# A hybrid attention and short-convolution block on one core: the order of its start, the steps of its attention, and how one row of scales is spread over the partitions

## The chip, the cores and the metric

The kernel runs on one core of a Trainium2 chip. The metric is the device time of one execution in microseconds. The engines are named as the profile names them: PE is TensorE (matmuls), PEld its weight load, DVE VectorE, ACT ScalarE, POOL GpSimd, and SP is SyncE, whose queue issues nearly all DMA transfers here. Each engine takes its own instructions in the order in which the program holds them, and one that waits holds up all that stand behind it on the same engine.

## The reference

One layer of a diffusion block over 512 latent tokens (width 2048) with 256 context tokens, everything in fp32:

```
mod_l = silu(c) @ w_ada + b_ada            # 6 x 2048 numbers: shifts, scales, gates
mod_c = silu(c_ctx) @ w_ada + b_ada
h_l = rms_norm(x, g) * (1 + sc_a) + sh_a   # h_c likewise from ctx
qa, kva, kr, cb, cc, ch = split(h @ w_in)
q = rms_norm(qa) @ w_q_b ;  k, v = rms_norm(kva) @ w_kv_b      # 8 heads, rotary part shared
att = softmax(q k^T * scale) v             # 512 queries, 768 keys
conv = cb * dwconv3(cc * ch)
x = x + gt_a * (rms_norm_per_128(concat(att, conv)) @ w_out)
hf = rms_norm(x) * (1 + sc_f) + sh_f
u = dwconv3(hf @ w_up); x = x + gt_f * ((a * silu(g)) @ w_down)
return rms_norm(x, g_final)
```

## The kernel before, in words

The activations lie transposed in the core's memory: 16 tiles of 128 features by 512 tokens. Every fp32 operand of a large product is split into a high part (a cast on ACT to the matmul's own 32-bit format, name ending in h) and a low part (a subtraction on DVE, name ending in l), and `mm3` makes three matmuls of each product, high by high, high by low and low by high (L170 to L172). So a weight block that has landed still needs one ACT and one DVE instruction before PE can use it whole.

**The start.** c lands, four matmuls spread it over the partitions, ACT applies silu to it (`silu_rows`), and sv holds it. Sixteen tiles of x (xr) land; ACT squares each (L317 ff.), DVE adds the squares into one tile xs0t (L318), and PE sums that over the partitions into rs (L283). In between PE and ACT do the same for c_ctx (tile cc, into svc). `rsqrt` takes the root on ACT and the reciprocal on DVE, `spread` (L264) turns the 512 numbers into a tile rl with equal rows: a matmul of a broadcast column with the identity for every 128 tokens. With rl each x tile j is scaled (`modulate`, L398), given its scale and shift (ACT, L401) and split into hj. The scale and shift of tile j are two of the 96 products of w_ada with sv: a *dot* is a DVE instruction over 128x1024 numbers that multiplies a landed half tile of w_ada with half of sv and sums it (`dot_v`, L216), so two halves for each product. The halves land in a ring of four buffers (tag ada), and SP issues all transfers in program order (`ordered`, L128), so a transfer behind a half waits until the dot that frees its buffer is done. The input projection runs over the 16 tiles in three chunks of k (2, 6 and 8 tiles; the names pf, rf, wf belong to a chunk's first columns, pp, rw, w to the others), and w_in comes in pieces of up to 1 MB in a ring of two buffers (tag raw, three in later parts).

**The attention** (from about 444 us) has 32 steps: a head and a quarter of the queries each. A step takes the row maximum of the scores from PSUM (DVE, L683), multiplies it by -scale (DVE, L684), applies exp (ACT, L687), transposes the six 128x128 blocks of the probabilities on PE (t, L700), splits them into pth (ACT, L703) and ptl (DVE, L704), computes scores two steps ahead, and every second step multiplies by the values (po). Beside that, each step does one *late dot* pair (ra, L238), loads the next 1 MB of w_ada for it in three of every four steps, does one eighth of the next head pair's projections (`pieces`), and fetches one step ahead the weights that this will use (rq, rk, `fetch`). After each head pair `merge` spreads eight groups of scales (gr) with the matmuls of L741 into gb; `gn_apply` (late_bg) does so for the convolution groups by `spread` (gn).

**After the last step** comes the output projection (of): its operands mx0 to mx15 are split (L300, L301), its first weights (ofr into ofw) are fetched and split, and dots go on (ada). Which instruction an engine takes next where the program leaves it open is set by the scheduler that builds the program; `keep` pins an instruction to program order.

Of the kernel before, what the change touches and what calls it, by code (L numbers as in the profile page):

```python
# [60 lines left out]
def block_kernel(ctx, tc, xt, ctxt, ctxn, c, c_ctx, w_ada, small, w_in, w_inc, w_q, w_kv, w_out,  # L61
# [67 lines left out]

    def fetch_to(dst, src):  # L130

        ins = SP.dma_start(dst, src)
        if ordered[0]:
            keep(ins)
# [10 lines left out]
    def split(raw, a, n, name):  # L145
# [7 lines left out]
        A.copy(out=hi[:, :n], in_=raw[:, a:a + n])  # L153
        V.tensor_tensor(out=lo[:, :n], in0=raw[:, a:a + n], in1=hi[:, :n].bitcast(F32), op=ALU.subtract)  # L154
# [53 lines left out]
    def total(col, t, dst):  # L208

        V.scalar_tensor_tensor(out=dst, in0=col[:, 0:1], scalar=col[:, 1:2], in1=s("b_ada", t), op0=ALU.add, op1=ALU.add)  # L210

    def dot_v(raw, vec, t, dst, nm):

        col = tiny(2, f"dv{nm}{t}")
        for i, r in enumerate(raw):
            V.scalar_tensor_tensor(out=r, in0=r, scalar=1.0, in1=vec[:, i * 1024:(i + 1) * 1024], op0=ALU.mult, op1=ALU.mult, accum_out=col[:, i:i + 1])  # L216
# [39 lines left out]
    def scale_of(dst, g, m):  # L256
        V.scalar_tensor_tensor(out=dst, in0=m, scalar=1.0, in1=g, op0=ALU.add, op1=ALU.mult)

    def rsqrt(r, ms, n):

        A.activation(r, ms, AF.Sqrt, bias=eps, scale=1.0 / n)
        V.reciprocal(r, r)

    def spread(pb, r):  # L264

        for g in range(r.shape[1]):
            PE.matmul(pb[:, g * P:(g + 1) * P], bc(r[:, g:g + 1], P), ident, start=True, stop=True)

    def rms_steps(sqs, n, a, width, dst, wait=0, one=False):
# [11 lines left out]
        for i, sq in enumerate(sqs):  # L281
            for g in range(ng):
                PE.matmul(ps[:, g:g + 1], sq[:, a + g * P:a + (g + 1) * P], ones[:, 0:1], start=i == 0 and g == 0, stop=i == len(sqs) - 1 and g == ng - 1)  # L283
# [5 lines left out]
        if dst is not None:  # L289
            A.copy(out=dst[:, a:a + width], in_=pb[:, :width])  # L290
        yield pb[:, :width]

    def rms(sqs, n, width, dst):
        for _ in rms_steps(sqs, n, 0, width, dst):
            pass

    def hilo(src, n, nm, width=512):
        hi = t2([P, width], F32R, nm + "h")
        lo = t2([P, width], F32R, nm + "l")
        A.copy(out=hi[:, :n], in_=src)  # L300
        V.tensor_tensor(out=lo[:, :n], in0=src, in1=hi[:, :n].bitcast(F32), op=ALU.subtract)  # L301
# [8 lines left out]
    def add_squares(total, x, n, nm, E=None, a=0, new=tmp):  # L310
        c = slice(a, a + n)
        if total is None:
            total = new([P, T], F32, nm + "t")
            A.activation(total[:, c], x, AF.Square)
            return total
        q = tmp([P, T], F32, nm)
        A.activation(q[:, :n], x, AF.Square)  # L317
        (E or V).tensor_tensor(out=total[:, c], in0=total[:, c], in1=q[:, :n], op=ALU.add)  # L318
# [44 lines left out]
    with ExitStack() as pa:  # L363
# [4 lines left out]
        def silu_rows(src, dst, nm):  # L368
# [3 lines left out]
            for g in range(4):  # L372
# [4 lines left out]
                A.activation(dst[:, g * 512:(g + 1) * 512], ps, AF.Silu)  # L377

        def ada_load(t):
            return ada_tiles(p_sb, 4, w_ada[t], f"ada{t}")  # L380

# [8 lines left out]

        def prep(j):
# [934 lines left out]
```

## Time and profile before

| | us |
|---|---|
| Median of 3 runs | 2210.82 |
| Lowest, highest | 2207.34, 2219.75 |
| The profiled execution: its time | 2206.8 |
| The profiled execution: its span | 2204.9 |
| Granted clock of PE in it | 0.996 |
| ACT, POOL busy | 1010.5, 111.3 |

The span is what the trace covers; 1.9 us of that execution's time lie outside it. The median of the runs lies 4.0 us above the profiled execution. A row of the timeline has the start, the length, the engine, the line, the operation, the tiles (result on the left of the arrow) and how many instructions it stands for, and in brackets the idle time ahead of it and what ended that. Matmuls overlap, so the length of one says less than the distance between the starts of two.

### The profile page before, as it was taken

To read this page: it belongs to the slowest core of one execution; us is meant where nothing else is said; L and a number is where in the kernel's file an instruction comes from. 1 tells how busy PE (TensorE), PEld (TensorE's weight loads), DVE (VectorE), ACT (ScalarE), POOL (GpSimd) and SP (SyncE) were. 2 spreads that over 40 slices of the span, in tenths; PEclk is the share of its full clock that TensorE was granted. 3 is DMA by queue.
4 is the path that set the end of the run, shared out by engine and by line. 5 is a ranking of instruction groups with operands and counts; after the bars stand their busy time and mean duration, and the time that the engine had idled before them with its cause. 6 is when DMAs were issued, how large, how long until landed. Compare 5 with 4: busy or idle time off the path is not lost.

```text
span 2204.9 us, 34542 instructions
## 1 busy us (share of the span) xinstructions
PE 2149.2 (97%) x13346; PEld 1914.2 (87%) x13346; DVE 1599.0 (73%) x2493; ACT 1010.5 (46%) x1635; POOL 111.3 (5%) x149
## 2 busy tenths in 40 slices
PE   7899999999999999999999999999999999999998
PEld 4688888878888888899999999999999888888887
DVE  7998887678896848777777777777777873633544
ACT  5523333544452237555554555555554432532444
POOL 0000000000000000011111011111110000000000
PEclk9999999999999999999999999999999999999999
DMA  8989884434469925577777777777776995753462
GB/s 331 344 276 334 275 279 150 144 120 149 158 235 358 331 86 172 132 196 201 204 194 195 201 205 195 194 201 201 201 193 200 350 345 159 247 164 92 160 210 88
DMA packets 144264, 466.75 MB, mean 212 GB/s; under 512 B 16290, under 2 KB 20642, under 8 KB 138082
## 3 DMA queue, kind: packets, MB, share of 16 engines
q1 hardware_dynamic: 125652, 405.03, 54.1%
q0 software_dynamic: 16272, 57.42, 12.8%
q8 instruction: 104, 1.70, 0.3%
q10 hardware_dynamic: 2176, 2.10, 0.3%
q14 instruction: 60, 0.49, 0.1%
HBM read 442.73 MB, written 20.71 MB: 210 GB/s over the span
## 4 chain that ended last, share of the span: by engine, by line
PE 91%; DVE 4%; DMA 2%; ACT 2%; issue 1%; SPq 0%; POOL 0%; DVEq 0%; ACTq 0%
PE d L170 7%; PE d L172 7%; PE d L171 7%; PE pp L170 4%; PE pp L172 4%; PE pp L171 4%; PE o L172 1%; PE o L171 1%; PE o L170 1%; PE uf L170 1%; PE uf L171 1%; PE uf L172 1%; PE of L172 1%; PE pf L171 1%; PE of L170 1%; PE of L171 1%
## 5 line engine op out<-in xcount | busy, mean ns | idle before, releaser
L997 POOL DMA_DIRECT2D u_s<-in_w_up x80 | 68.1, 851 | 416.3 <-DMA u_s<-in_w_up 353.4
L153 ACT CAST w_0h<-rw 128x512 fp32r<-128x512 f32 (+1 forms) x63 | 38.5, 618 | 107.3 <-PE pp L171 65.7
L216 DVE SCALAR_TENSOR_TENSOR ada<-ada,sv 128x1024 f32<-128x1024 f32 x64 | 77.4, 1217 | 4.6 <-DMA ada<-in_w_ada 4.6
L491 DVE SCALAR_TENSOR_TENSOR ada<-ada,svc 128x1024 f32<-128x1024 f32 x64 | 75.9, 1218 | 2.0 <-DMA ada<-in_w_ada 1.8
L238 DVE SCALAR_TENSOR_TENSOR ra<-ra,sv 128x1024 f32<-128x1024 f32 x50 | 59.4, 1216 | 0.0
L154 DVE TENSOR_TENSOR w_0l<-rw,w_0h 128x512 fp32r<-128x512 f32 (+1 forms) x63 | 42.4, 680 | 21.8 <-ACT w_0h L153 21.8
L238 DVE SCALAR_TENSOR_TENSOR ada<-ada,sv 128x1024 f32<-128x1024 f32 x46 | 55.7, 1218 | 2.6 <-DMA ada<-in_w_ada 2.6
L1108 DVE TENSOR_TENSOR u<-u,u 128x1024 f32<-128x1024 f32 x40 | 49.0, 1225 | 1.3
L1107 DVE TENSOR_TENSOR u<-u,u_s 128x1024 f32<-128x1024 f32 x40 | 48.7, 1217 | 0.0
L939 POOL DMA_DIRECT2D y_d<-a x43 | 24.7, 576 | 386.2 <-DVE a L938 376.7
L732 POOL TENSOR_TENSOR gr<-gr,half 128x8 f32<-128x8 f32 x4 | 8.3, 2084 | 641.4 <-DVE mx L684 505.3
L238 DVE SCALAR_TENSOR_TENSOR adl<-adl,sv 128x1024 f32<-128x1024 f32 x32 | 38.8, 1218 | 0.2 <-DMA adl<-in_w_ada 0.2
L683 DVE TENSOR_REDUCE mx<-s 128x1 f32<-128x768 f32 x32 | 30.4, 951 | 8.4 <-PE s L673 8.4
L704 DVE TENSOR_TENSOR ptl<-t,pth 128x384 fp32r<-128x384 f32 x64 | 33.2, 548 | 4.2 <-ACT pth L703 4.2
L502 DVE TENSOR_TENSOR acc<-acc,pp 128x512 f32<-128x512 f32 x50 | 33.9, 678 | 1.9 <-PE pp L172 1.8
L703 ACT CAST pth<-t 128x384 fp32r<-128x384 f32 x64 | 28.5, 488 | 14.3 <-PE t L700 14.1
L936 ACT ACTIVATE g<-g 128x512 f32<-128x512 f32 x43 | 27.2, 633 | 12.1 <-DVE g L930 12.1
L928 ACT ACTIVATE g<-cg,sm 128x512 f32<-128x512 f32 x40 | 32.5, 813 | 0.0
L687 ACT ACTIVATE p<-s,mx 128x768 f32<-128x768 f32 x32 | 29.3, 915 | 6.8 <-DVE mx L684 6.6
L928 ACT ACTIVATE a<-ca,sm 128x512 f32<-128x512 f32 x40 | 32.1, 802 | 0.0
L700 PE MATMUL t<-io,p 128*128 128x128 f32 x192 | 27.5, 274 | 3.7 <-ACT p L687 2.4
L929 DVE SCALAR_TENSOR_TENSOR g<-cg,sm,g 128x511 f32<-128x511 f32 x40 | 29.8, 745 | 0.0
(15580 smaller groups left out, 8734.8 us busy)
## 6 DMA issues: line engine op xcount, KB each, us to landing
ada<-in_w_ada SPq DMA_DIRECT2D x174, 512.0 KB, 6.0
u<-in_w_up SPq DMA_DIRECT2D x120, 512.0 KB, 8.3
u_s<-in_w_up SPq DMA_DIRECT2D x80, 512.0 KB, 4.1
u_s<-in_w_up POOLq DMA_DIRECT2D x80, 512.0 KB, 9.5
d<-in_w_dn SPq DMA_DIRECT2D x86, 384.0 KB, 3.8
y<-y_d SPq DMA_DIRECT2D x129, 256.0 KB, 4.5
ra<-in_w_ada SPq DMA_DIRECT2D x25, 1024.0 KB, 4.8
adl<-in_w_ada SPq DMA_DIRECT2D x32, 512.0 KB, 6.0
```

The lines of the kernel that those rows point to most:

```text
L153: A.copy(out=hi[:, :n], in_=raw[:, a:a + n])
L154: V.tensor_tensor(out=lo[:, :n], in0=raw[:, a:a + n], in1=hi[:, :n].bitcast(F32), op=ALU.subtract)
L170: PE.matmul(ps, w[0], x[0], start=first, stop=False, skip_group_check=on_top)
L171: PE.matmul(ps, w[0], x[1], start=False, stop=False, skip_group_check=on_top)
L172: PE.matmul(ps, w[1], x[0], start=False, stop=last, skip_group_check=on_top)
L216: V.scalar_tensor_tensor(out=r, in0=r, scalar=1.0, in1=vec[:, i * 1024:(i + 1) * 1024], op0=ALU.mult, op1=ALU.mult, accum_out=col[:, i:i + 1])
L238: keep(V.scalar_tensor_tensor(out=r, in0=r, scalar=1.0, in1=svs[i], op0=ALU.mult, op1=ALU.mult, accum_out=lc[:, t % 4:t % 4 + 1] if i else ...
L491: keep(V.scalar_tensor_tensor(out=raw[q], in0=raw[q], scalar=1.0, in1=svc[:, q * 1024:(q + 1) * 1024], op0=ALU.mult, op1=ALU.mult, accum_o ...
L928: A.activation(u, src, AF.Identity, bias=s("fb", m), scale=s("fw", 86 + m))
L997: G_.dma_start(r[-1], src[more], accum_op=ALU.add)
L1107: V.tensor_tensor(out=a11, in0=a11, in1=s1, op=ALU.add)
L1108: V.tensor_tensor(out=a12, in0=a12, in1=a11, op=ALU.add)
```

## The change

It has six parts.

1. **Spreads.** `spread` issues a PE transpose of the broadcast column where it had a matmul with the identity. `merge` now calls `spread` too.
2. **The start.** The dots of tiles 0 and 1 (products 16, 0, 17, 1) get buffers of their own, four quarters of 128x512 each, with quarters' dots (`ada_quarter`); those of 16 land ahead of x, those of 0, 17 and 1 after the first weights. DVE's, ACT's and SP's order in this stretch is written out and pinned (`pin`). The squares are added in groups of five tiles (xs0t, xs5t, xs10t, xs15t), and PE sums each group over the partitions as it is done. A small silu and the constant sm come early; a root no longer stands between.
3. **c_ctx.** The PE spread of c_ctx is gone. After the first weights of chunk 1 (rf12) a DMA broadcasts c_ctx to all partitions (128x2048, 1 MB), and one ACT silu of 128x2048 makes svc of it.
4. **A root and exp tables.** A tiny exp after the last root of the stretch before the attention.
5. **Softmax.** g_q is multiplied by -scale once, so that the scores come out negated and scaled; the step takes the row minimum, and the multiplication L684 goes.
6. **Steps.** The first q_nope of the second pair is done ahead of the loop, weights are fetched up to two steps ahead, and the late loads stand in steps 2 to 7 of every eight, so that steps 0 and 1 have none and the dots of steps 1 and 2 of every eight are gone.
The diff, cut to its core:

```diff
@@ spread, rms_steps
-            PE.matmul(pb[:, g * P:(g + 1) * P], bc(r[:, g:g + 1], P), ident, start=True, stop=True)
+            PE.transpose(pb[:, g * P:(g + 1) * P], bc(r[:, g:g + 1], P), ident)
@@ the start
+        def ada_quarters(t):
+            r = []
+            for i in range(4):
+                r.append(t2([P, T], F32, f"aq{t}{i}"))
+                fetch_to(r[i], w_ada[t][:, i * T:(i + 1) * T])
+            return r, tiny(4, f"dq{t}")
...
+        fetch_to(sm, small)
+        quarters = {16: ada_quarters(16)}
         xs = []
-        for j in range(NK):
-            xs.append(t2([P, T], F32, f"xr{j}"))
-            fetch_to(xs[j], xt[:, j * T:(j + 1) * T])
-            ssq = add_squares(ssq, xs[j], T, f"xs{j}")
-        silu_rows(c_ctx, svc, "cc")
-        fetch_to(sm, small)
-        rms([ssq], D, T, rl)
+        def squares():
+            for j in range(NK):
+                xs.append(t2([P, T], F32, f"xr{j}"))
+                fetch_to(xs[j], xt[:, j * T:(j + 1) * T])
+                ssq = add_squares(ssq if j % 5 else None, xs[j], T, f"xs{j}")
+                if j in (1, 3, 5):
+                    next(silus)
+                if j in (6, 8, 11, 13):
+                    ada_quarter(16)
+                if j % 5 == 4 or j == NK - 1:
+                    yield ssq
+        rms(squares(), D, T, rl, 4)
+        first_raw = load(w_in[:, :2 * G * P], 2 * G * P, "rf00")
+        quarters.update({t: ada_quarters(t) for t in (0, 17, 1)})
+        ada_quarter(0)
+        first_w = blocks(first_raw, 4, "wf00")
+        ada_quarter(0)
+        normed(0)
+        ada_quarter(0)
+        ada_quarter(0)
+        modulate(0)
+        first_w += blocks(first_raw, 8, "wf04", 4)
+        for t in (17, 1):
+            for _ in range(4):
+                ada_quarter(t)
+        normed(1)
+        modulate(1)
@@ after chunk 1's first columns
+                fetch_to(svc, c_ctx.to_broadcast([P, D]))
+                A.activation(svc, svc, AF.Silu)
                 fetch_to(kc, consts[:, :KCW])
@@ softmax
-            V.tensor_reduce(mx, ss[:, :768], axis=AX.X, op=ALU.max)
-            V.tensor_scalar(mx, mx, scalar1=-SCALE, scalar2=None, op0=ALU.mult)
+            V.tensor_reduce(mn, ss[:, :768], axis=AX.X, op=ALU.min)
-            A.activation(pt, ss[:, :768], AF.Exp, bias=mx, scale=SCALE, accum_out=den[hd // 2][:, i:i + 1])
+            A.activation(pt, ss[:, :768], AF.Exp, bias=mn, scale=-1.0, accum_out=den[hd // 2][:, i:i + 1])
@@ the attention's loop
-            if n % 4 != 3:
-                late_load(ada_raw)
-            if pr < 3:
-                f, p_, i = pieces(pr + 1)[n % 8]
-                f(p_, i)
-                if n + 1 < 24:
-                    fetch((n + 1) // 8 + 1, (n + 1) % 8)
+            at = n % 8
+            if at == 0 and n and n < 24:
+                fetch(pr + 1, 1)
+            if pr < 3 and n:
+                f, p_, i = pieces(pr + 1)[at]
+                f(p_, i)
+            if at < 2 and n < 24:
+                fetch(pr + 1, 2 + at)
+            elif at >= 2:
+                late_load(ada_raw)
+                if at == 6 and n < 16:
+                    fetch(pr + 2, 0)
```

The order of the instructions follows. The first place is DVE between the reciprocal of the root and the low part of tile 0 (h0l). aq and ada are pieces of w_ada under a dot, wf the split first weights, xr the x tile scaled by rl. Before:

```order
L262 RECIPROCAL rr<-rr 128x4
L154 TENSOR_TENSOR wf_0l<-rf_249,wf_0h 128x512
L154 TENSOR_TENSOR wf_4l<-rf_249,wf_4h 128x512
L154 TENSOR_TENSOR wf_8l<-rf_249,wf_8h 128x512
L398 TENSOR_TENSOR xr_112<-xr_112,rl 128x512
L216 SCALAR_TENSOR_TENSOR ada_281,dvl_285<-ada_281,sv 128x1024
L301 TENSOR_TENSOR h0l<-xr_112,h0h 128x512
```

In the changed kernel the same stretch of DVE reads:

```order
L279 RECIPROCAL rr<-rr 128x4
L415 SCALAR_TENSOR_TENSOR aq_233,dq_241<-aq_233,sv 128x512
L165 TENSOR_TENSOR wf_0l<-rf_231,wf_0h 128x512
L415 SCALAR_TENSOR_TENSOR aq_235,dq_241<-aq_235,sv 128x512
L430 TENSOR_TENSOR xr_118<-xr_118,rl 128x512
L415 SCALAR_TENSOR_TENSOR aq_237,dq_241<-aq_237,sv 128x512
L415 SCALAR_TENSOR_TENSOR aq_239,dq_241<-aq_239,sv 128x512
L417 TENSOR_TENSOR dq_241<-dq_241 128x2
L221 SCALAR_TENSOR_TENSOR mod<-dq_241,sm 128x1
L270 SCALAR_TENSOR_TENSOR sc_271<-mod,sm 128x1
L321 TENSOR_TENSOR h0l<-xr_118,h0h 128x512
```

The four dots of product 0 moved from ahead of the reciprocal to behind it, and two of them stand between the scaling of x and the scale sc that tile 0 needs.

The second place is DVE after the attention: from the last ptl (the last low part of a transposed block) to the first low weights of the output projection, ofw_0l. Before, all that stands between is this:

```order
L704 TENSOR_TENSOR ptl_5856<-t_5902,pth_5855 128x3x128
L301 TENSOR_TENSOR mx2l<-acc_393,mx2h 128x512
L301 TENSOR_TENSOR mx3l<-acc_423,mx3h 128x512
L243 TENSOR_TENSOR mod<-mod,lc 128x4
L238 SCALAR_TENSOR_TENSOR ra_5894,mod<-ra_5894,sv 128x1024
L244 TENSOR_TENSOR mod<-mod,sm 128x4
L238 SCALAR_TENSOR_TENSOR ra_5894,lc<-ra_5894,sv 128x1024
L154 TENSOR_TENSOR ofw_0l<-ofr_5997,ofw_0h 128x512
```

In the changed kernel 33 instructions stand between the two: the low parts mx1l to mx13l, six dots of ra, four of ada, the scalings of four acc and two o by gb, and four of a few numbers each. The last twelve rows up to ofw_0l read:

```order
L321 TENSOR_TENSOR mx7l<-acc_736,mx7h 128x512
L820 SCALAR_TENSOR_TENSOR o_5707<-o_5707,sm,gb_5970 128x512
L251 SCALAR_TENSOR_TENSOR ada_6061,mod<-ada_6061,sv 128x1024
L321 TENSOR_TENSOR mx8l<-o_4126,mx8h 128x512
L820 SCALAR_TENSOR_TENSOR o_5866<-o_5866,sm,gb_5976 128x512
L321 TENSOR_TENSOR mx9l<-o_4384,mx9h 128x512
L251 SCALAR_TENSOR_TENSOR ada_6063,lc<-ada_6063,sv 128x1024
L321 TENSOR_TENSOR mx10l<-o_4673,mx10h 128x512
L321 TENSOR_TENSOR mx11l<-o_4931,mx11h 128x512
L321 TENSOR_TENSOR mx12l<-o_5222,mx12h 128x512
L321 TENSOR_TENSOR mx13l<-o_5480,mx13h 128x512
L165 TENSOR_TENSOR ofw_0l<-ofr_5995,ofw_0h 128x512
```

The split of the first output weights moved behind the splits of nearly all operands and behind eight more dots.

The third place is PE at the same point. Before, two groups of spreads (gb) are left, and of starts with a piece whose low weights follow at once. Now all spreads stand ahead and these rows follow:

```order
L284 MATMUL gb_5976<-io,gr_5941 128x128 x4
L181 MATMUL of_5990<-mx0h,ofw_0h 128x512
L182 MATMUL of_5990<-mx0l,ofw_0h 128x512
L181 MATMUL of_5991<-mx0h,ofw_0h 128x512
L182 MATMUL of_5991<-mx0l,ofw_0h 128x512
L181 MATMUL of_5994<-mx0h,ofw_4h 128x512
L182 MATMUL of_5994<-mx0l,ofw_4h 128x512
L181 MATMUL of_5992<-mx0h,ofw_0h 128x512
L182 MATMUL of_5992<-mx0l,ofw_0h 128x512
L181 MATMUL of_5993<-mx0h,ofw_0h 128x512
L182 MATMUL of_5993<-mx0l,ofw_0h 128x512
L183 MATMUL of_5990<-mx0h,ofw_0l 128x512
```

Ten matmuls moved ahead of the first one that needs ofw_0l. On ACT the broadcast's silu stands, with a table load ahead of it, between the casts wf_0h and wf_4h of chunk 1's last first weights (rf12).

96 lines of the change are left out of this document (65 added, 31 removed).

## The prediction

> **What bounds the kernel now.** I read the page first, then the windows, then the waits of PE by stretch, and last the timelines of the two places at which the change puts DVE's work in another order. From the page come the busy times and the chain that ended last:
>
> ```profile
> PE 2149.2 (97%) x13346; PEld 1914.2 (87%) x13346; DVE 1599.0 (73%) x2493; ACT 1010.5 (46%) x1635; POOL 111.3 (5%) x149
> PE 91%; DVE 4%; DMA 2%; ACT 2%; issue 1%; SPq 0%; POOL 0%; DVEq 0%; ACTq 0%
> ```
>
> PE is the bound: whatever shortens its own work or ends its waits shows in full, and whatever only relieves DVE shows nothing, unless PE waits for DVE. The windows (microseconds, then busy time and count of PE, PEld, DVE, ACT and POOL, PE's clock, DMA share, GB/s) tell where PE is not dense:
>
> ```profile
> 0.00:30.00 30.00, 18.55 (x32) 8.25 (x32) 19.48 (x35) 20.91 (x35) 0.20 (x4) 1.00 0.95 356
> 85.00:410.00 325.00, 323.23 (x1429) 261.70 (x1428) 282.56 (x543) 119.48 (x216) 0.00 (x0) 1.00 0.75 259
> 410.00:636.00 226.00, 212.26 (x1448) 191.56 (x1446) 179.12 (x353) 112.49 (x244) 5.79 (x3) 1.00 0.43 148
> 636.00:670.00 34.00, 32.81 (x171) 27.73 (x172) 34.00 (x62) 14.39 (x26) 2.55 (x1) 0.95 0.87 311
> ```
>
> From 85 us to the attention PE is full, so a start that ends later by some microseconds stays late. Up to 636 us it idles 226.00 - 212.26 = 13.7 us; behind that DVE is busy all 34 us of its window. PE's waits between 410 and 670 us (total, times, longest):
>
> ```profile
> PE s L669 <- ACT p L687: 3.4, 3, 1.5
> PE t L700 <- ACT p L687: 2.4, 2, 2.1
> PE pq L172 <- DVE wq12l L154: 1.3, 1, 1.3
> PE pq L170 <- ACT wq11h L153: 0.9, 1, 0.9
> PE qr L342 <- ACT xq L591: 0.7, 1, 0.7
> PE pq L170 <- ACT wq21h L153: 0.5, 1, 0.5
> ```
>
> **Term 1, the start: +6 us.** The timelines of DVE, ACT and PE around the root:
>
> ```profile
> 18.09 1.49 DVE L318 TENSOR_TENSOR xs0t<-xs0t,xs 128x512 f32<-128x512 f32 x2
> 22.73 1.87 PE L283 MATMUL rs<-io,xs0t 128*128 128x1 f32 x8
> 27.38 0.59 ACT L290 COPY rl<-rs 128x512 f32<-128x512 f32 x1 [0.83 <-PE rs L267]
> 28.00 0.69 DVE L398 TENSOR_TENSOR xr<-xr,rl 128x512 f32<-128x512 f32 x1 [0.56 <-ACT rl L290]
> 28.73 0.81 ACT L401 ACTIVATE xr<-xr,mod,sc 128x512 f32<-128x512 f32 x1 [0.76 <-DVE xr L398]
> 29.57 0.62 ACT L300 CAST h0h<-xr 128x512 fp32r<-128x512 f32 x1
> 30.24 2.08 PE L170 MATMUL pf<-h0h,wf_0h 128*128 128x512 f32 x4 [2.90 <-ACT h0h L300]
> ```
>
> The adds end at 19.58; PE, still at the spread of c_ctx, comes to the sum at 22.73. Without that spread the sum would start with the last add. But ahead of x now come 1 MB of quarters and the constants, some 1.3 MB, at the 356 GB/s of the first window 3.5 us; I put the last add at 22 (19.6 if x had slack, 23 if all 3.5 count). Two groups of sums are left then, 2 x 1.87, and root, reciprocal, spread and copy take 27.97 - 24.60 = 3.4 less some 0.8 for the shorter spread (term 3): with 22 + 3.74 + 2.6 rl is ready at 28.3, 0.4 later than before. From rl to the first matmul it was 30.24 - 27.97 = 2.3. Now DVE has ahead of sc the rows of the order: wf_0l, whose cast waits behind the copy of rl (0.6 each; the scaling's row has 0.69, of which some 0.1 overlaps the next), a dot of 512 (0.6, half of the 1.15 below), the scaling 0.6, two dots 1.2, and 0.5 of small ones: 4.1 us; with 0.81 and 0.62 on ACT that is 5.5. So the first matmul comes at 33.8, +3.6.
>
> What PE waits for next is the ring. The rows of the twelfth half dot, and of the cast and matmul that wait for the transfer behind it:
>
> ```profile
> 42.90 1.22 DVE L216 SCALAR_TENSOR_TENSOR ada<-ada,sv 128x1024 f32<-128x1024 f32 x1
> 44.05 0.08 DVE L216 DVE_READ_ACCUMULATOR ada<-ada,sv 128x1 f32 x1
> 52.96 0.62 ACT L153 CAST w_0h<-rw 128x512 fp32r<-128x512 f32 x1 [5.43 <-DMA rw<-in_w_in]
> ```
>
> The second rw is issued after that dot, and lands 8.9 us on. In the changed order it still stands behind the same 12 halves (16 quarters and four halves), of which only four quarters lie ahead of the root. Behind h0l (34.5) DVE has two wf low parts (1.2), eight quarters (4.6), small ones 0.4, a scaling 0.6, then waits for ACT's scale and cast (1.4), h1l 0.6, a w low part 0.6 and four halves with two more low parts (5.8): the twelfth half is done at about 50, against 44.1. That gives +6; +2 if the transfers are early and the scheduler's estimate of them is what put the dots there, +7 if x is as late as it can be.
>
> **Term 2, c_ctx: +2 us.** The spread was PE work in a stretch where PE waited, so its absence is in term 1. The broadcast and its silu come at the worst place of ACT's queue:
>
> ```profile
> 22.83 0.60 ACT L377 ACTIVATE svc<-cc 128x512 f32<-128x512 f32 x1 [1.11 <-PE cc L376]
> 23.45 1.28 ACT L261 ACT_TABLE_LOAD   x1
> 86.50 0.62 ACT L153 CAST wf_0h<-rf 128x512 fp32r<-128x512 f32 x1 [0.57 <-DMA rf<-in_w_in]
> 90.46 0.40 PE L170 MATMUL pf<-h5h,wf_4h 128*128 128x512 f32 x1
> ```
>
> PE takes wf_4h at 90.46. The silu's 1 MB lands about 1 MB / 0.356 = 2.9 us after rf12, its four times 512 take about 1.9 (an estimate, from 0.60 each less the fixed part), the table 1.28 hides in the landing: wf_4h is ready at 86.5 + 2.9 + 1.9 + 0.6 = 91.9, 1.4 too late, and with the copies of four accumulators that queue behind it I take +2 (0 if the transfer lands with rf12, +4 if the table comes on top).
>
> **Term 3, spreads: -10 us.** The distance of starts in a pair of rows each, PE's timeline:
>
> ```profile
> 508.21 0.82 PE L700 MATMUL t<-io,p 128*128 128x128 f32 x6
> 508.78 0.48 PE L669 MATMUL s<-kl11h,q11h 128*128 128x512 f32 x1
> 510.61 1.95 PE L741 MATMUL gb<-io,gr 128*128 128x128 f32 x16
> 512.31 0.48 PE L170 MATMUL pq<-qa0h,wq22h 128*128 128x512 f32 x1
> ```
>
> Six transposes take 0.57, so 95 ns each. Sixteen instructions are eight spreads (an fp32 matmul is two instructions), 1.70, so 213 ns each: 118 ns less by transposing. The lines view counts them:
>
> ```profile
> L267 PE MATMUL gb<-io,gn x64: 270/275/421, 442.6 to 643.4; 128*128 128x128 f32 x64
> L741 PE MATMUL gb<-io,gr x64: 270/275/376, 510.6 to 652.0; 128*128 128x128 f32 x64
> L267 PE MATMUL rs<-io,rr x44: 270/275/581, 25.3 to 2195.4; 128*128 128x128 f32 x44
> ```
>
> 128 instructions of gb are 64 spreads: 7.5 us. Of rs, 22 spreads less the four of the start: 2.1 us. All lie on PE's path or at the end of a chain that PE waits for. The Trainium skill, "TensorE: Matmul & The Clock Gate", Part 4, says that a transpose does not count as busy time for the clock gate and costs some 275 ns in a kernel. By the length column the trace agrees (270 to 275 ns for either), but the starts show the price, and the window of 410 to 636 us has 192 transposes at a granted clock of 1.00. By that page's 275 ns against the 213 of the rows, 82 spreads would cost 5 us more instead of 10 less, an estimate; the rows decide here.
>
> **Term 4, waits in the attention: -9 us.** Of the rows of waits above, those for p (3.4 and 2.4, the second with a table load of exp of 1.28), for wq (1.3, 0.9, 0.5) and for xq (0.7) are what the change goes at: 9.2 in all. They end if the minimum goes straight to exp and the weights are there; what is late next is ptl, since DVE is busy 179.12 of 226.00 us and some 18 us of PE time would go. I take 9; -4 if only the weights' waits and the table load end (2.7 + 1.3), -11 if the small ones go too.
>
> **Term 5, the junction to the output projection: +9 us.** PE's, DVE's and ACT's rows:
>
> ```profile
> 630.57 1.17 PE L700 MATMUL t<-io,p 128*128 128x128 f32 x6
> 636.41 0.55 DVE L704 TENSOR_TENSOR ptl<-t,pth 128x384 fp32r<-128x384 f32 x1
> 638.15 1.22 DVE L238 SCALAR_TENSOR_TENSOR ra<-ra,sv 128x1024 f32<-128x1024 f32 x1
> 640.52 0.68 DVE L154 TENSOR_TENSOR ofw_0l<-ofr,ofw_0h 128x512 fp32r<-128x512 f32 x1
> 642.04 0.48 PE L170 MATMUL of<-mx0h,ofw_4h 128*128 128x512 f32 x1
> 652.33 0.39 PE L171 MATMUL of<-mx0l,ofw_0h 128*128 128x512 f32 x1
> 652.56 0.39 PE L172 MATMUL of<-mx0h,ofw_0l 128*128 128x512 f32 x1
> ```
>
> Before, ofw_0l starts 4.1 us after the last ptl does. Now 33 instructions stand between: 13 low parts and six scalings of 512 numbers (0.6), ten dots (1.15) and four small ones (0.1), together 23.3 us, and with its own 0.7 the weights come 24 us after ptl. ptl itself comes earlier against PE: the last transposes started at 630.57, and DVE, with dots ahead, came to ptl at 636.41; now it should follow them within a microsecond. Counting in before's clock, ptl is done at 632.6, ofw_0l at 656.5. In before PE has by then worked on of since 642.04, 14.5 us, less some 5 for the spreads and sums that its order holds in between: 9.5 us of matmuls, 41 at 0.23. In the changed order it has done ten, so it is 31 x 0.23 = 7.2 us back. After a wait PE is slow at first: behind its 2.90 us at the start four matmuls took 2.08 instead of 0.92, so I add 1.5. If DVE is as late as before it is 3.8 us more, and with as much again for what then queues, +15; +3 if the scalings and dots fall into waits that DVE has anyway. I take +9.
>
> **The sum** is 6 + 2 - 10 - 9 + 9 = -2 us. Against the profiled execution's 2206.8 that is 2204.8; the median of the runs lies 4.0 above it, so I forecast 2209. About 0.5%, 11 us, is what a measurement of this kernel can tell from no change, so the forecast is no change, with large terms of both signs.
>
> **The rivals.**
>
> *Faster: the start costs nothing.* The transfers ahead of the dot at 42.90 are early, or the dots run while DVE would wait, so terms 1 and 2 are 0, the waits' term is at -11 and the junction at 7.2: -10 - 11 + 7.2 = -13.8, 2197. For it speaks that DVE idles 10.5 of the first 30 us, against it that the four dots of product 0 stand behind the root in DVE's order. It decides if the first matmul of h0 comes by 31 and that of chunk 1 not after 86.
>
> *Slower: DVE becomes the bound of the last attention steps.* ptl queues behind dots, so waits for p turn into waits for ptl (0 instead of -9), and the junction takes its +15: 6 + 2 - 10 + 0 + 15 = 13, 2224. For it: DVE is 100% busy from 636 us already; against: before the attention's last steps it had 47 us of slack in 226. It decides if ofw_0l comes more than 27 us after the last transposes.
>
> *The spreads give nothing.* If a transpose of a broadcast column costs what the matmul did, the sum is +8: 2219. Against it stand the 95 ns of t. With the page's price of term 3 it would be 2224.
>
> *The clock falls at the spreads.* By the mechanism that sixteen transposes in a row leave PE counted as idle, each of eight groups of spreads would be followed by matmuls at the cold interval, and cost what the row at 30.24 shows, 2.08 - 0.92 = 1.2 us a group: some +9, with the forecast's -2 +7, 2218. The windows speak against it. The Trainium skill's Part 4, named above, is the rule for it.
>
> **How the numbers follow.** Forecast 0.43, start free 0.29, DVE bound 0.17, spreads nothing 0.05, clock 0.06. Faster by over 0.5%: the 0.29 and 0.04 of the forecast's own lower tail, 0.33. Slower: 0.17, 0.03 of the forecast's upper tail and 0.02 of the last two, 0.22. Within: 0.45. The lower bound takes in the free start with the upper gains of term 3 and 4, 2192; the upper one the bound DVE, 2224; beyond each lies about a tenth.
>
> **What would show it.** Right: first matmul of h0 at about 34 us and of chunk 1 some 6 us later than 84.9; gb at 95 ns; no wait of PE for wq; a wait of PE of about 10 us for ofw_0l. Wrong: chunk 1 at 85 or earlier, no wait at ofw_0l, or more than 12 us of waits left between 410 and 636.

## The result, and the profile after

The changed kernel takes 2232.03 us (median of 6 runs, 2229.14 to 2238.89) against 2210.65 us (6 runs): a ratio of 1.0099, 95% interval [1.0071, 1.0126]. It is about 21 us slower, where the forecast was 2209 and no change. The profiled execution took 2234.48 us, with a span of 2232.7. The page's busy times, then the windows, in the columns named before:

```profile
PE 2151.6 (96%) x13274; PEld 1924.3 (86%) x13274; DVE 1596.1 (71%) x2479; ACT 1014.3 (45%) x1635; POOL 112.9 (5%) x149
```

```profile
0.00:30.00 30.00, 15.88 (x44) 10.05 (x44) 11.72 (x28) 15.33 (x27) 0.20 (x4) 1.00 0.95 350
85.00:410.00 325.00, 318.12 (x1390) 256.34 (x1389) 281.38 (x541) 122.91 (x216) 0.00 (x0) 0.99 0.78 267
410.00:636.00 226.00, 218.09 (x1451) 196.96 (x1450) 178.43 (x323) 118.29 (x254) 7.54 (x3) 0.99 0.42 146
636.00:670.00 34.00, 21.61 (x89) 17.33 (x88) 34.00 (x64) 14.01 (x27) 2.62 (x1) 0.70 0.88 329
```

PE's busy time hardly moved: spreads are shorter, but more matmuls ran at a slow clock and one stretch of the FFN was longer. The span grew by 28, so nearly all of it is idle time of PE, and the windows say where: PE idles 7.9 us from 410 to 636 us where it idled 13.7 before, but 12.4 us of the 34 behind it where it idled 1.2, and its mean clock there is 0.70 and not 0.95. Six of PE's waits of the whole kernel are new or longer and bear on the terms of the sum (total, times, longest):

```profile
PE u3a L181 <- DVE a L1018: 10.8, 1, 10.8
PE gb L284 <- POOL gr L810: 7.8, 4, 3.4
PE pf L181 <- ACT h0h L319: 6.4, 1, 6.4
PE of L183 <- DVE ofw_0l L165: 3.6, 1, 3.6
PE of L181 <- ACT ofw_0h L164: 3.0, 1, 3.0
PE pf L181 <- ACT wf_4h L164: 2.7, 1, 2.7
```

How late each kernel is against the one before, at matmuls that both have, tells more than any total. The table gives, from PE's timelines, the start in the kernel before and the delay in the others (the experiments are described below):

| matmul | before | changed | start alone | attention alone | spreads alone | late loads back |
|---|---|---|---|---|---|---|
| first of h0 | 30.2 | +5.2 | +6.3 | -0.5 | -0.9 | +5.5 |
| first of chunk 1 (h2) | 84.9 | +8.9 | +11.9 | -0.3 | -0.1 | +8.2 |
| first pp of chunk 1 | 103.1 | +13.4 | +14.3 | -0.4 | -0.2 | +11.1 |
| first scores | 436.2 | +14.8 | +15.6 | -1.0 | -1.3 | +12.3 |
| last po | 640.2 | +2.7 | +21.2 | -10.0 | +6.1 | +2.9 |
| last of | 714.1 | +16.6 | +21.1 | +4.2 | +4.2 | +2.2 |
| first uf | 831.8 | +16.3 | +21.1 | +3.8 | +4.1 | +2.3 |
| first u5a | 939.4 | +22.0 | +26.6 | +3.6 | +3.8 | +8.2 |
| first u40a | 1637.1 | +29.8 | +26.6 | +11.5 | +3.8 | +8.2 |

So in the changed kernel the start costs 8.9, chunk 1's entry 4.5 (and 1.4 more up to the first scores), the attention gives 12.1 back, the stretch behind it costs 13.9, and a place in the FFN that the prediction did not look at 5.7. The 7.8 us from u5a to u40a go with no edit: the profiled executions of all these kernels take either 697.8 us or 705.6 there, and that of the changed kernel is of the second kind.

The rows that answer to those of before. At the start, DVE, PE and SP:

```profile
23.08 0.68 DVE L338 TENSOR_TENSOR xs10t<-xs10t,xs 128x512 f32<-128x512 f32 x1
23.82 1.86 PE L300 MATMUL rs<-io,xs10t 128*128 128x1 f32 x8 [2.41 <-DVE xs10t L338]
27.72 0.18 DVE L279 RECIPROCAL rr<-rr 128x4 f32<-128x4 f32 x1 [3.96 <-ACT rr L277]
30.24 0.69 DVE L165 TENSOR_TENSOR wf_0l<-rf,wf_0h 128x512 fp32r<-128x512 f32 x1 [1.76 <-ACT wf_0h L164]
33.74 0.15 DVE L270 SCALAR_TENSOR_TENSOR sc<-mod,sm 128x1 f32<-128x1 f32 x1
35.44 2.50 PE L181 MATMUL pf<-h0h,wf_0h 128*128 128x512 f32 x5 [6.37 <-ACT h0h L319]
52.97 0.60 SPq L142 DMA_DIRECT2D rw<-in_w_in  x1
```

The last add of squares ends at 23.8, and PE's third sum waits 2.41 us for it: the fourth dot of product 16 and two small instructions stand pinned ahead of this add, from 22.02 on. Then DVE idles 3.96 us until the root, and works the pinned rows up to sc at 33.74 before ACT can scale tile 0. The second rw is issued at 52.97; before, it was this row:

```profile
44.58 0.38 SPq L132 DMA_DIRECT2D rw<-in_w_in  x1
```

At chunk 1, ACT:

```profile
97.62 0.81 ACT L443 ACTIVATE xr<-xr,mod,sc 128x512 f32<-128x512 f32 x1 [1.21 <-DVE xr L430]
98.45 1.28 ACT L622 ACT_TABLE_LOAD   x1
99.75 1.91 ACT L622 ACTIVATE svc<-svc 128x2048 f32<-128x2048 f32 x1
101.56 0.60 ACT L164 CAST wf_4h<-rf 128x512 fp32r<-128x512 f32 x1
```

The broadcast, issued at 87.76, landed 10.5 us later, at 98.3. The table load is not hidden by it: in ACT's queue it stands behind an xr that waits for DVE until 97.62, and so its 1.28 and the silu's 1.91 both delay wf_4h. Behind the attention, DVE and PE:

```profile
638.34 1.02 DVE L782 TENSOR_TENSOR ptl<-t,pth 128x384 fp32r<-128x384 f32 x2
662.78 0.71 DVE L165 TENSOR_TENSOR ofw_0l<-ofr,ofw_0h 128x512 fp32r<-128x512 f32 x1
650.63 1.97 PE L284 MATMUL gb<-io,gr 128*128 128x128 f32 x8 [3.44 <-POOL gr L810]
655.64 0.80 PE L181 MATMUL of<-mx0h,ofw_0h 128*128 128x512 f32 x1 [3.05 <-ACT ofw_0h L164]
663.55 2.08 PE L183 MATMUL of<-mx0h,ofw_0l 128*128 128x512 f32 x4 [3.63 <-DVE ofw_0l L165]
```

From the last ptl to ofw_0l it is 23.4 us from end to start (23.3 were counted). PE meets three waits in a row, for POOL's root, for ofr's landing and for ofw_0l, and after each it starts at half clock: these four matmuls start 0.43 us apart, where 0.23 is the distance at full clock. The second of the three waits comes from SP's queue. The first ofr was issued at 634.78 before (the first row, which holds two transfers); now it stands behind ra loads, and these wait for DVE's dots:

```profile
634.78 6.18 SPq L132 DMA_DIRECT2D ofr<-in_w_out_first  x2
634.10 8.59 SPq L142 DMA_DIRECT2D ra<-in_w_ada  x3
645.85 0.33 SPq L142 DMA_DIRECT2D ofr<-in_w_out_first  x1
```

### The profile page after: what moved, and what is told of

It is laid out like the page before. It is cut to its first block, busy times and chain, and to the rows that moved or that the text cites. A ratio compares the mean times of both kernels' runs of the same rounds, so it can differ in the third digit from the quotient of the medians.

```text
span 2232.7 us, 34380 instructions
## 1 busy us (share of the span) xinstructions
PE 2151.6 (96%) x13274; PEld 1924.3 (86%) x13274; DVE 1596.1 (71%) x2479; ACT 1014.3 (45%) x1635; POOL 112.9 (5%) x149
## 4 chain that ended last, share of the span: by engine, by line
PE 90%; DVE 4%; DMA 2%; ACT 2%; issue 1%; POOL 0%; SPq 0%; DVEq 0%; ACTq 0%; POOLq 0%
PE d L181 7%; PE d L182 7%; PE d L183 7%; PE pp L181 3%; PE pp L182 3%; PE pp L183 3%; PE o L182 1%; PE o L183 1%; PE o L181 1%; PE of L183 1%; PE of L181 1%; PE of L182 1%; PE pf L181 1%; PE uf L181 1%; PE uf L182 1%; PE uf L183 1%
## 5 line engine op out<-in xcount | busy, mean ns | idle before, releaser
L227 DVE SCALAR_TENSOR_TENSOR ada<-ada,sv 128x1024 f32<-128x1024 f32 x56 | 67.9, 1229 | 2.7 <-DMA ada<-in_w_ada 2.6
L251 DVE SCALAR_TENSOR_TENSOR ada<-ada,sv 128x1024 f32<-128x1024 f32 x46 | 55.3, 1224 | 5.4 <-DMA ada<-in_w_ada 5.3
L165 DVE TENSOR_TENSOR w_0l<-rw,w_0h 128x512 fp32r<-128x512 f32 (+1 forms) x63 | 43.1, 690 | 21.5 <-ACT w_0h L164 21.2
L762 DVE TENSOR_REDUCE mn<-s 128x1 f32<-128x768 f32 x32 | 30.4, 955 | 8.8 <-PE s L751 8.6
L765 ACT ACTIVATE p<-s,mn 128x768 f32<-128x768 f32 x32 | 29.3, 915 | 2.7 <-DVE mn L762 1.8
L1018 DVE SCALAR_TENSOR_TENSOR a<-ca,sm,a 128x511 f32<-128x511 f32 x40 | 29.9, 747 | 0.0
```

Source lines behind the costliest of these rows:

```text
L165: pin(V.tensor_tensor(out=lo[:, :n], in0=raw[:, a:a + n], in1=hi[:, :n].bitcast(F32), op=ALU.subtract))
L227: ins = V.scalar_tensor_tensor(out=r, in0=r, scalar=1.0, in1=vec[:, i * 1024:(i + 1) * 1024], op0=ALU.mult, op1=ALU.mult, accum_out=col[:, ...
L251: keep(V.scalar_tensor_tensor(out=r, in0=r, scalar=1.0, in1=svs[i], op0=ALU.mult, op1=ALU.mult, accum_out=lc[:, t % 4:t % 4 + 1] if i else ...
L1018: V.scalar_tensor_tensor(out=u[:, :T - 1], in0=src[:, 1:], scalar=s("fw", 172 + m), in1=u[:, :T - 1], op0=ALU.mult, op1=ALU.add)
```

## The experiments

My theory after these rows was that four things cost time, each by itself: the start's order, c_ctx's silu, the late loads' new places, and a PSUM bank at u3a; and that spreads and the attention's waits are true gains. The rivals stand with each run. Each ratio is against the kernel before on the same chip; a difference between two of the other kernels is taken from their ratios or medians.

**Spreads alone** (e1_spreads), on the kernel before:

```diff
-            PE.matmul(pb[:, g * P:(g + 1) * P], bc(r[:, g:g + 1], P), ident, start=True, stop=True)
+            PE.transpose(pb[:, g * P:(g + 1) * P], bc(r[:, g:g + 1], P), ident)
```

> The kernel before with the spreads by transposes alone, in the start, the norms and the merges. If a transposed spread costs what the transposes of the probabilities do (95 ns against 213) the time falls by 8 to 10 us, and the 16 instructions of gb at a merge become 8 that take 0.8 us. The rival, that transposes let PE's clock fall: no gain or up to 9 us lost, with half-clock stretches behind the merges. A third: the spread is hidden behind the wait for POOL's gr, then 4 us or less.

Measured: 2214.33 against 2208.67, ratio 1.0022 [1.0009, 1.0036]: 5 us slower. Neither the gain nor quite the rival: up to the scores it is 1.3 us ahead, and in the attention it loses 7.4. PE's waits there:

```profile
PE t L700 <- ACT p L687: 8.0, 3, 4.4
PE pq L170 <- ACT wq31h L153: 2.8, 1, 2.8
PE pq L170 <- ACT wq21h L153: 2.4, 1, 2.4
```

In the kernel before these were 2.4, nothing and 0.5. To the first exp PE comes 3.4 us earlier (at 444.2 for 447.6) and exp only 1.1, so the wait grows. The weights are later than before: wq21h's cast starts at 530.89 for 528.66, wq31h's at 585.44 for 580.50. These three rows grew by 10.3, but others shrank, and in all PE idles only 3.0 us more from 410 to 636. The larger part of the loss is PE's clock, 0.97 there where it was 1.00:

```profile
410.00:636.00 226.00, 209.22 (x1375) 187.99 (x1375) 173.44 (x339) 107.83 (x234) 5.79 (x3) 0.97 0.41 144
```

A mean of 0.97 over 226 us is some 14 us at half speed, an estimated 7 us lost. Three slow stretches stand right behind these waits: the clock is 0.57 from 449 to 453 us, 0.57 from 531 to 535 and 0.66 from 585 to 590. Behind the merges, whose transposes start at 513.4, 568.2 and 620.3, it is 1.00. So the clock did fall, but not where the rival has it.

**The start alone** (e2_start): the changed kernel with the old spreads, softmax and attention loop.

```diff
-            PE.transpose(pb[:, g * P:(g + 1) * P], bc(r[:, g:g + 1], P), ident)
+            PE.matmul(pb[:, g * P:(g + 1) * P], bc(r[:, g:g + 1], P), ident, start=True, stop=True)
...
-            V.tensor_reduce(mn, ss[:, :768], axis=AX.X, op=ALU.min)
+            V.tensor_reduce(mx, ss[:, :768], axis=AX.X, op=ALU.max)
+            V.tensor_scalar(mx, mx, scalar1=-SCALE, scalar2=None, op0=ALU.mult)
...
-            if at < 2 and n < 24:
-                fetch(pr + 1, 2 + at)
-            elif at >= 2:
+            if n % 4 != 3:
                 late_load(ada_raw)
```

> The kernel before with the new start and the new c_ctx alone (old spreads, old attention). My reading of the trace of the changed kernel: the start costs 8.5 us at the second rw, the silu of c_ctx ahead of wf_4h some 5 more, and the first product after the first FFN columns (u3a) gets a PSUM bank that DVE still reads, 5.5 us more: 17 to 20 us slower, with u3a waiting for DVE by 10 us. The rival, that the u3a wait comes from the attention's part or from DVE being late since the junction: 13 us, u3a without a wait.

Measured: 2234.72, ratio 1.0118 [1.0101, 1.0135], 26 us slower. At the scores it is 15.6 behind, and u3a has the same wait:

```profile
PE u3a L181 <- DVE a L1006: 10.8, 1, 10.8
```

So the wait at u3a comes with the start. Beyond what I expected, the attention, unchanged in the code, lost another 5.6 us. About 5 of them are the clock again: 0.83 from 460 to 470 us and 0.67 from 490 to 500, where the kernel before has 1.00 from 440 to 500. The wait for p ahead of the first of these is 2.1 us long in both kernels, and only here a slow stretch follows it.

**The attention alone** (e3_attention): the kernel before with the new softmax, exp table, loop and weights.

```diff
-            V.tensor_reduce(mx, ss[:, :768], axis=AX.X, op=ALU.max)
-            V.tensor_scalar(mx, mx, scalar1=-SCALE, scalar2=None, op0=ALU.mult)
+            V.tensor_reduce(mn, ss[:, :768], axis=AX.X, op=ALU.min)
...
+        with tc.issue_after(roots[0]), tc.issue_after(roots[1]):
+            A.activation(tiny(1, "exp"), eps, AF.Exp)
...
+        q_nope(1, 0)
+        fetch(1, 1)
...
-            if n % 4 != 3:
+            if at < 2 and n < 24:
+                fetch(pr + 1, 2 + at)
+            elif at >= 2:
                 late_load(ada_raw)
```

> The kernel before with the new softmax, the exp table, the weights two steps ahead and the late loads' new places alone (old spreads and start). If the junction's loss comes from these late loads: waits -8 and junction +14, 4 to 8 us slower, with PE waiting for ofw_0l and half-clock stretches from about 640 us. The rival, that the start or the transposes bring the junction's loss: 6 to 10 us faster and no wait for ofw_0l.

Measured: 2215.19, ratio 1.0023 [1.0004, 1.0041]. It gains 9.0 us from the first scores to the last po and loses 14.2 up to the last of. The window behind the attention, 636 to 670 us, and three of PE's waits between 600 and 720 us:

```profile
636.00:670.00 34.00, 25.38 (x96) 20.23 (x96) 30.23 (x56) 12.37 (x23) 2.55 (x1) 0.80 1.00 373
```

```profile
PE gb L746 <- POOL gr L737: 3.4, 2, 2.9
PE of L170 <- DVE o L748: 2.6, 1, 2.6
PE of L172 <- DVE ofw_0l L154: 1.7, 1, 1.7
```

The junction's loss belongs to this part; start and transposes don't need to be there. PE's clock is 0.80.

**Another order of PSUM banks** (e4_banks), on the changed kernel:

```diff
-BANKS = [0, 1, 7, 4, 5, 6, 2, 3]
+BANKS = [2, 3, 7, 4, 5, 6, 0, 1]
```

> The changed kernel with one line different: the order in which the FFN takes the eight PSUM banks starts with banks 2 and 3 instead of 0 and 1. If the wait of 10.8 us at u3a is for a bank alone, it goes, and with it the half-clock stretch behind it: 5 to 8 us faster than the changed kernel, so 13 to 16 us slower than the kernel before. The rival, that DVE is simply late there and the next product waits instead: no change, 21 us slower.

Measured: 2221.80, ratio 1.0069 [1.0053, 1.0085], by the ratios 7 and by the medians 10 us faster than the changed kernel. In the FFN's first stretch the wait of 10.8 is gone and the one of the kernel before stands there:

```profile
PE u3c L181 <- ACT u3q5h L1009: 4.3, 1, 4.3
```

Its delay stays at 16.3 to 16.6 from uf to u40a. So u3a's wait was for its bank.

**Late loads back** (e5_late), on the changed kernel:

```diff
-            elif at >= 2:
+            if n % 4 != 3:
                 late_load(ada_raw)
+            if at >= 2:
                 if at == 6 and n < 16:
```

> The changed kernel with the late loads back in three of every four steps, all else as changed. If these places put DVE's dots behind the attention and ofw_0l behind them, the junction's 14 us go (in the order 6 instructions stand between the last ptl and ofw_0l again instead of 33): 10 to 14 us faster than the changed kernel, 8 to 12 slower than the kernel before, with no wait for ofw_0l. The rival, that the dots in the loop then delay ptl and the minimum again: the attention loses what the junction gains, within 4 us of the changed kernel.

Measured: 2213.85, ratio 1.0020 [1.0003, 1.0038], 17 us faster than the changed kernel. The junction costs nothing any more (+2.9 at the last po, +2.2 at the last of), and the attention keeps 9.4 of its 12.1. Its window behind the attention:

```profile
636.00:670.00 34.00, 29.80 (x147) 24.35 (x148) 34.00 (x63) 15.72 (x30) 2.55 (x1) 0.95 0.91 339
```

DVE is as full as ever there; what differs is what it does first. SP issues the first ofr at 638.11 again, not 645.85. This run moves all late loads back and not the last ones alone, so which of them matter it does not tell.

**c_ctx in the start again** (e6_cctx), on the changed kernel, behind the last square:

```diff
-                fetch_to(svc, c_ctx.to_broadcast([P, D]))
-                A.activation(svc, svc, AF.Silu)
...
+                if j == NK - 1:
+                    for _ in silu_rows(c_ctx, svc, "cc"):
+                        pass
```

> The changed kernel with c_ctx spread and put through silu in the start again, by PE and four ACT instructions ahead of the sum, and without the broadcast of 1 MB and its silu later. If the silu ahead of wf_4h costs 4 to 5 us, chunk 1 and 2 stand 9 us behind the kernel before and not 14: 3 to 5 us faster than the changed kernel. The rival, that c_ctx in the start delays the root by as much (1.7 us of the kernel before's PE work would stand behind the last square): no change.

Measured: 2232.43, ratio 1.0094 [1.0072, 1.0116], as the changed kernel. Both were half right. Its first matmul of h0 comes 9.4 us later than the changed kernel's, far more than I allowed for the rival:

```profile
44.81 1.65 PE L181 MATMUL pf<-h0h,wf_0h 128*128 128x512 f32 x3 [6.37 <-ACT h0h L319]
```

Between the first matmul of chunk 1 and the first pp it falls back by nothing against the kernel before (+18.6 at both), the changed kernel by 4.5, and the wait for wf_4h is gone. So the silu's place costs 4.5, and its absence from the start is worth more than that against this placement.

**Attention with the old late loads** (e7_att_late), the third experiment with the edit of the fifth:

```diff
-            elif at >= 2:
+            if n % 4 != 3:
                 late_load(ada_raw)
```

> The kernel before with the new softmax, the exp table and the weights two steps ahead, but with the late loads where they were; old spreads, old start. The attention alone gave 9 to 10 us up to the last po and lost 14 behind it. If the late loads made only the loss: 8 to 10 us faster than the kernel before. The rival, that they made the gain too: no change.

Measured: 2201.62, ratio 0.9970 [0.9950, 0.9989], 7 us faster.

**The same with spreads** (e8_att_late_spreads):

```diff
-            PE.matmul(pb[:, g * P:(g + 1) * P], bc(r[:, g:g + 1], P), ident, start=True, stop=True)
+            PE.transpose(pb[:, g * P:(g + 1) * P], bc(r[:, g:g + 1], P), ident)
```

> The same with the spreads by transposes. Alone these lost 5 us, with the waits of the old attention longer by what PE saved. If the waits for exp and for weights were what took the gain, it appears here: 4 to 7 us faster than the run without them, so 12 to 16 faster than the kernel before. The rival, that transposes lower PE's clock or that POOL's gr ends each merge anyway: no change against the run without them, or slower.

Measured: 2195.97, ratio 0.9927 [0.9907, 0.9947], 13 us faster by the medians, 16 by the ratio. Here the spreads give 6 us by the medians and 9 by the ratios, where alone they lost 5. PE's waits from 436 to 670 us, where those for wq are gone:

```profile
PE gb L270 <- POOL gr L737: 3.4, 2, 2.6
PE s L674 <- ACT p L692: 2.6, 3, 1.5
PE po L171 <- DVE ptl L709: 2.2, 1, 2.2
```

**The dots of product 0 ahead of the root** (e9_dots), on the changed kernel:

```diff
                     yield ssq
+            first["raw"] = load(w_in[:, :2 * G * P], 2 * G * P, "rf00")
+            quarters.update({t: ada_quarters(t) for t in (0, 17, 1)})
+            for _ in range(4):
+                ada_quarter(0)
+            first["w"] = blocks(first["raw"], 4, "wf00")
...
-        ada_quarter(0)
-        first_w = blocks(first_raw, 4, "wf00")
-        ada_quarter(0)
         normed(0)
-        ada_quarter(0)
-        ada_quarter(0)
         modulate(0)
```

> The changed kernel with the four dots of product 0 and the first weight split ahead of the reciprocal of the root, where the trace of the changed kernel has DVE idle for 4.0 us. If these dots behind the root are what holds the first matmul back, it comes at about 32 instead of 35.4 us, the second rw some 3 us earlier, and the time falls by 3 to 4 us against the changed kernel. The rival, that the ring of ada halves or the transfers set the pace from there on: the first matmul comes earlier, the first matmul of chunk 1 does not, and the time stays.

Measured: 2227.43, ratio 1.0072 [1.0047, 1.0096]; 4.6 us under the changed kernel by the medians, though the intervals of the two overlap. The trace shows what the edit does at the start:

```profile
32.78 1.65 PE L181 MATMUL pf<-h0h,wf_0h 128*128 128x512 f32 x3 [2.97 <-ACT h0h L319]
```

2.7 us earlier at h0, 3.6 at chunk 1, 3.2 at the scores. So the order of these dots is 3.6 of the start's 8.9. At the last po only 0.2 of that is left, and at u5a the two kernels stand level (+22.2 and +22.0). Most of this is the clock: both wait 1.9 us for gr ahead of a merge at about 570 us, and behind the same wait one runs at full speed and the other does not. The first row is the changed kernel's, the second this run's:

```profile
566.00:580.00 14.00, 12.11 (x75) 10.17 (x74) 9.74 (x18) 6.04 (x13) 2.48 (x1) 1.00 0.47 162
566.00:580.00 14.00, 12.10 (x58) 10.01 (x57) 8.81 (x16) 6.06 (x13) 2.48 (x1) 0.76 0.52 191
```

0.76 over 14 us is some 3.4 us lost. Whether the whole kernel gains what its start does, this run alone does not show.

**Three repairs together** (e10_three): the changed kernel with the edits of the fourth, fifth and ninth.

```diff
-BANKS = [0, 1, 7, 4, 5, 6, 2, 3]
+BANKS = [2, 3, 7, 4, 5, 6, 0, 1]
...
+            for _ in range(4):
+                ada_quarter(0)
...
-            elif at >= 2:
+            if n % 4 != 3:
                 late_load(ada_raw)
```

> The changed kernel with three things undone or mended: the late loads where they were, the other order of PSUM banks, and the dots of product 0 ahead of the root. If the parts add up (late loads -17 as measured, banks -6 to -10, dots -3) it is at 2200 to 2206, 3 to 9 us faster than the kernel before. The rival, that one takes what the other gives: within 4 us of the run with the late loads alone, 2210 to 2214.

Measured: 2204.25, ratio 0.9974 [0.9958, 0.9990], some 6 us faster than the kernel before: they add up within the noise. Against the run with the late loads alone it is 2.9 us earlier at the scores and 4.5 at the first uf (-2.2 for +2.3), so here the dots' gain lasts. At the scores it is still 9.4 us late; the rest of the start's order and c_ctx are in it.

**Spreads and weights only** (e11_spreads_weights): the kernel before with the transposes, the first q_nope and the fetches of the new loop, the late loads as before, and nothing else.

```diff
+            PE.transpose(pb[:, g * P:(g + 1) * P], bc(r[:, g:g + 1], P), ident)
...
+        q_nope(1, 0)
+        fetch(1, 1)
...
+            if at == 0 and n and n < 24:
+                fetch(pr + 1, 1)
+            if pr < 3 and n:
+                f, p_, i = pieces(pr + 1)[at]
+                f(p_, i)
+            if at < 2 and n < 24:
+                fetch(pr + 1, 2 + at)
             if n % 4 != 3:
                 late_load(ada_raw)
+            if at >= 2:
+                if at == 6 and n < 16:
+                    fetch(pr + 2, 0)
```

> The kernel before with the spreads by transposes and the weights two steps ahead, but with the old softmax, no early exp table and the late loads where they were. The spreads alone had waits for wq of 7.6 us and for p of 8 in the attention. If the spreads' gain was lost in the waits for weights, these end: 2 to 6 us faster than the kernel before. The rival, that it was lost in the wait for the first exp and the multiplication ahead of it: no faster than the spreads alone, 2 to 5 us slower than the kernel before.

Measured: 2195.47, ratio 0.9932 [0.9907, 0.9958], 15 us faster: as fast as the eighth, which has the new softmax and the exp table too. PE's largest wait in the attention is still that for p:

```profile
PE t L700 <- ACT p L687: 6.5, 3, 3.9
```

So the first exp's wait is not what took the gain of the spreads: it stands here as it did, and the gain is there. What took it ended with the weights' fetch. But the step from the spreads alone to this run is 19 to 21 us, more than the spreads can save, so part of it is the fetch's own; no run has the fetch alone. The softmax's part gave nothing that can be measured beside it. The eighth and this kernel beat both the kernel before and the changed one.

## Why the prediction was wrong, point by point

The forecast's mechanisms were nearly all there; four sizes were off, all to the same side, and one place was not looked at. Of the signs named for right, h0 came at 35.4 for 34, no wait for wq was left, and PE did wait for ofw_0l, but 3.6 us and not 10. The median lies 8 us above the range.

- **Term 1, +6.** 8.9 at chunk 1's first matmul. rl came at 29.7 instead of 28.3, h0 at 35.4 instead of 33.8, the second rw at 53.0 instead of some 50. The chain by the ring held; its parts were each a little short. The size that failed first is the last add, put at 22 and ended at 23.8, behind a pinned dot of product 16. The four dots of product 0 behind the root were counted; the ninth run shows their place at 2.7 to 3.6 us.
- **Term 2, +2.** 4.5 by the table and by the sixth run. The step that failed is "the table 1.28 hides in the landing". The landing was sized well (98.3, 2.5 us behind the cast of rf12 at 95.8, where 2.9 were taken), but ACT came to the table load at 98.45, behind the xr that waits for DVE, so all of it lay behind the landing. My own upper end had this.
- **Terms 3 and 4, -10 and -9.** 12.1 came between the scores and the last po. The waits for wq did go. What took their place was not ptl but POOL's gr: 4.3 us in three waits up to the last po (and 3.4 in a fourth behind it), where the kernel before has none up to there and 1.0 behind it. The price of a spread was nearly right: the eight at 571.58 take 0.84 us up to the next matmul, 105 ns each. That the two terms add, and that all spreads lie on PE's path, were assumptions, and the runs show how they fail: the spreads alone lose 5 us, with the weights ahead they are part of 15. The rival that spreads give nothing thus holds for the old loop, though not for its reason: a transposed spread is shorter, and PE then waits and runs at half clock behind the waits.
- **Term 5, +9.** 13.9. The count of DVE's rows was right (23.4 us against 23.3). What failed is the price of PE's side: that ptl follows its transposes within one us (638.34 against the last t at 635.66, so 2.7), one wait instead of three, and 1.5 us of slow clock. I had looked at DVE's and PE's order and not at SP's queue, where ofr moved back by 11 us. With PE at 0.70 over 34 us, at half speed while it is slow, 0.6 of the window or 20 us was slow, in part waiting and in part matmuls at 0.43 us. The fifth run shows that the late loads' places cause all of it. The row from which I took the 1.5 does not show a clock that falls after a wait: the spread ahead of that wait, at 25.27, was as slow (eight instructions 0.21 us apart, against 0.106 at 510.61), so PE had not been at full clock yet.
- **Left out: u3a, +5.7.** The term was at nothing because I had read the order up to the output projection only. In the kernel before, PE's largest wait there is this:

```profile
PE u3c L170 <- ACT u3q5h L921: 4.3, 1, 4.3
```

With the new start u3a waits 10.8 us instead, for DVE's rows of a, which read the tiles of uf. The second run shows that it comes with the start and the fourth that it is the bank. The sixth and the ninth still have it, so neither c_ctx nor the dots of product 0 bring it; which step of the start does stays open.

- **The rivals.** The slower one named DVE as the bound behind the attention, and gave 2224. ofw_0l came 27 us after the last transposes, at its point of decision; but the waits of the attention did go, so it is right in the place and wrong in the trade. The clock rival is wrong in its place: in the first run, the spreads alone, the clock is 1.00 behind the merges and low behind waits, and in the runs with transposed spreads and the weights ahead the spreads' gain is measured. What is left of it is that the clock costs more than the sum allows for, an estimated 7 us in the first run's attention. For the rule of the Trainium skill, "TensorE: Matmul & The Clock Gate", Part 4, no run here shows a slower clock by transposes alone. None excludes it either: in the changed kernel a half-clock stretch at 639 us stands behind three waits of 0.3 to 0.8 us with six transposes between them.

A lesson in size, which is my reading and not shown by a run: terms of both signs were summed as independent, with errors as independent. Yet most costs were chains through a full DVE or a waiting PE, and the errors of these had one sign.

## What to carry to other kernels

An edit that frees time on the bound engine pays only if what that engine waits for next is earlier too: spreads alone lost 5 us, and were part of a gain of 15 with the weights' fetch ahead. When loads with follow-up work are moved towards the end of a stretch, look at what is queued behind their work in the next stretch, on the engine that does the work and in the queue that issues the transfers; here six loads of every eight steps moved by one or two steps towards the end, and 14 us were lost behind the loop. Compare the waits of the order over the whole program, also where the code is the same: buffers that rotate carry a change hundreds of microseconds on.

## What the runs showed of the hardware that was not expected

After its wait of 10.83 us at u3a PE's clock was 0.62 in the window of the wait (916 to 927 us) and 0.81 in the next 14 us:

```profile
916.00:927.00 11.00, 0.58 (x3) 0.15 (x1) 10.14 (x15) 5.82 (x8) 1.14 (x2) 0.62 0.30 96
927.00:941.00 14.00, 13.59 (x95) 13.62 (x96) 5.08 (x7) 3.69 (x5) 0.54 (x1) 0.81 0.30 94
```

0.81 over 14 us is 5.3 us at half speed, 2.7 us lost behind the wait. The Trainium skill, "TensorE: Matmul & The Clock Gate", Part 1, has about 3.4 us to warm up. Here it was somewhat more.

A wait does not have one price. Behind the wait of 1.9 us for gr at about 570 us the clock over 14 us was 1.00 in the changed kernel, 0.88 in the fourth and the sixth run and 0.76 in the ninth, so between nothing and 3.4 us were lost behind the same wait. A difference of 3 us between two single traces can be this alone.

The FFN's stretch from u5a to u40a, with not one wait on PE, took 697.8 us in ten profiled executions and 705.6 in three (the changed kernel's, the third and the sixth run's), a difference of 1.1% at a granted clock of 1.00. It is spread evenly over the 35 groups, 19.94 against 20.16 us each. No edit goes with it, and its cause is open.
